# Scores of a head in six products, and half of an output projection side by side with two pairs of K tiles by seven products

## The chip, the cores and the metric

The kernel runs on one NeuronCore of a Trainium2 chip. Its engines run their own instruction streams and meet at semaphores: TensorE (PE in the profile, with PEld for its weight loads), VectorE (DVE), ScalarE (ACT), GpSimd (POOL) and SyncE (SP), which here does nothing but issue DMAs. The metric is the device time of one execution in microseconds (us); the times given are medians over runs. Single instructions, waits and transfers are read from the trace of one profiled execution, whose own time stands beside its span.

## What is computed

Two layers of a decoder over 256 tokens of width 2048, in float32:

```python
for l in range(DEPTH):                       # DEPTH = 2
    h = _rmsnorm(x, attn_norm_g[l])
    proj = h @ w_in[l]                       # q | k | v | gate_b | gate_c | conv_in, 1024 each
    q, k, v, gate_b, gate_c, conv_in = jnp.split(proj, splits, axis=-1)
    q = _rmsnorm(q.reshape(B, S, N_HEADS, 2, HEAD_DK), q_norm_g[l])      # 8 heads, 2 x 64
    k = _rmsnorm(k.reshape(B, S, N_HEADS, 2, HEAD_DK), k_norm_g[l])
    ...
    # per head two score matrices s_m = q_m k_m^T * scale + bias, causal softmax each,
    # p = p_0 - lam * p_1, then p @ v, norm, scale
    attn = _diff_attention(q, k, v, lam, rel_bias)
    ...
    conv = gate_b * _short_conv(gate_c * conv_in, conv_w[l])
    x = x + jnp.concatenate([attn, conv], axis=-1) @ w_out[l]            # 2048 x 2048
    hm = _rmsnorm(x, mlp_norm_g[l]) @ w_up[l]
    x = x + jnp.square(jax.nn.relu(hm)) @ w_down[l]
```

## The kernel before

**Products.** A float32 number is carried as two float32r tiles, a high part (a ScalarE copy that rounds) and a low part (a VectorE subtraction of the high part). A product of two such matrices is three matmuls, high x high, high x low and low x high (`TERMS`). In `linear` (L386, matmuls at L399) 128 rows of the contraction (a K tile) take 2 x 3 = 6 matmuls of 512 columns: two token blocks `t`, three terms. The chunk of 512 output columns accumulates in a pair of PSUM banks, a `mm2` tile; there are two such tiles (pool `mm`), taken in turn. Three more banks go by `bank(...)` and one by the tag `av`.

**Weights.** `Weights` (L300) holds a list of jobs, made by `plain` (L346). A job issues a load of 512 KB (two K tiles by 512 columns, tile `raw`, four buffers) on SP's queue and splits it: `whi` on ScalarE (L315), `wlo` on VectorE (L316), three buffers each. `take` (L370) makes jobs up to three ahead of the one in use. `work` (class `Background`) advances attention and norms by ticks between matmuls.

**Order of a layer's mixer** (L730). q, k, v of half the heads; the attention of those heads runs in ticks beside the next products; the same for the other half. Then gate C and the convolution input (`gc`, `ci`, `linear_t`, L405), then gate B (`gb`, four products of 256 columns of the model). After each gate B product, `joined` evicts it (a ScalarE copy `gb3l` at L435, a VectorE sum `gb3w` at L437), `gate` (L724) multiplies it with the convolution into `ys` (L726) and `in_parts` (L717) splits it into a part of `cat` (L720, L721). `cat` has four tiles of four K tiles each: two from attention, two from the gates. Then the output projection, chunk after chunk: `o` of chunk n is `linear` over all 16 K tiles, added into `xs[n]` at L800, and the norm of that chunk starts (`Norm.chunk`, transposes at L469).

**Scores** (`unit`, L609). For a head, q and k are held with both 64-wide halves m: `kT` has the high part of k in half m's rows and again in the other half's, `kL` has the low part and zeros, `qT[:, m]` has the high part in its own 64 rows and the low part in the other 64. So for each m and each token block t a product with `kT` and one with `kL` give the score: 8 matmuls, of 128 columns for t = 0 and 256 for t = 1.

**What sets the order.** TensorE's order is that of the program. VectorE, ScalarE, SP and GpSimd are put in order by the tile framework's scheduler when the program is built; each runs its list in order. SP's list holds the loads of the next stage too: two 1 MB loads of the MLP's weights (`uraw`, L830) stand in it after the eighth load of the projection; their memory is that of mixer tiles, and they wait for the last reader of `ys`, the `cat` split at L721 of the fourth gate B product.

**The MLP** (L838 on) already holds a scheme of seven products; it isn't touched.

Of the kernel before, what the change touches and what calls it, by code (L numbers as in the profile page):

```python
# [9 lines left out]
F32 = mybir.dt.float32  # L10
# [5 lines left out]
P = 128  # L16
# [19 lines left out]
NB2 = DFF // (KG * P)  # L36

# [81 lines left out]
def trunk(ctx: ExitStack, tc: tile.TileContext, x, w_in, w_out, conv_w, q_norm_g, k_norm_g,  # L119
# [19 lines left out]
    def bank(name):  # L139
        return ps.tile([P, CH], F32, tag="bank", name=name)  # L140
# [307 lines left out]
    class Norm:  # L448
# [59 lines left out]
        def factors(self):  # L508
# [7 lines left out]
            diag = small.tile([P, NT, P], F32, tag="diag", name="diag", bufs=1)  # L516
# [82 lines left out]
    def attention(l, qT, kT, kL, v, h0, dst, bias, tmp, pace):  # L599
# [9 lines left out]
        def unit(i):  # L609
            h = h0 + i  # L610
            s = tmp.tile([P, 2, 3 * P], F32, tag="s", name=f"s{h}", bufs=2)
            mx = small.tile([P, NT, 2], F32, tag="mx", name=f"mx{h}")
            su = small.tile([P, NT, 2], F32, tag="su", name=f"su{h}")
            sc = [bank(f"sc{h}_{m}") for m in range(2)]
            for flip in range(2):
                for k in (kT, kL):
                    for t in range(NT):
                        W, m = (t + 1) * P, t ^ flip
                        nc.tensor.matmul(
                            sc[m][:, OFF[t]:OFF[t] + W], qT[:, m, i, t * P:(t + 1) * P],  # L620
                            k[:, m, i, :W], start=(k is kT), stop=(k is kL))
            for t in range(NT):
                W = (t + 1) * P
                for m in range(2):
                    nc.vector.tensor_tensor_reduce(
                        out=s[:, m, OFF[t]:OFF[t] + W], in0=sc[m][:, OFF[t]:OFF[t] + W],
                        in1=bias[:, 2 * h + m, S - W:], op0=ALU.add, op1=ALU.max, scale=1.0,
                        scalar=-3.0e38, accum_out=mx[:, t, m:m + 1])
# [100 lines left out]

    def mixer(l, norm, loads):  # L730

        with ExitStack() as scope:
# [17 lines left out]
            for n in range(D // CH):  # L750
                weights.straight(w_out[l], 0, D // P, n * CH)
# [10 lines left out]
            for half in range(2):  # L762
# [10 lines left out]
                for t in range(NT):  # L773
# [5 lines left out]
                                     1 + half), 3 + 9 * half)  # L779
# [17 lines left out]
            for n in range(D // CH):  # L797
# [8 lines left out]
    A11, A21, A12, A22, S1, S2, S3, S4 = range(8)  # L806
# [480 lines left out]
```

## Time and profile before

| | |
|---|---|
| median of 3 runs | 2129.5 us (2128.94 to 2129.52) |
| profiled execution, own time | 2129.46 us |
| its span in the trace | 2127.7 us |
| instructions in the trace | 29217 |
| matmuls | 10919, TensorE busy 2122.8 us |
| VectorE, ScalarE busy | 1692.9 us (80%), 1355.9 us (64%) |
| output projection | from 299.4 to 389.4 us in layer 0, from 1357 us in layer 1 |

A row of groups reads: line of the kernel, engine, operation, tile written <- tiles read, shapes, count | busy us, mean ns of one | idle us of the engine just before them and who ended it. A row of a timeline reads: start us, length us, engine, line, operation, tiles, count, and in brackets the idle time before it and its releaser. A row of the chain reads: start, length, engine, tile, line, count. A row of DMA issues reads: tile, queue, count, KB each, us to landing. Matmuls overlap in their pipeline: the 389 ns of one are its latency, and the spacing of starts is what it costs.

### The profile page before, as it was taken

How to read it: one execution, taken by the hardware profiler on the slowest of the kernel's cores; microseconds unless marked ns; L12 is line 12 of the kernel's file. 1: busy time of each engine (PE TensorE's matmuls, PEld its weight loads, DVE VectorE, ACT ScalarE, POOL GpSimd, SP SyncE). 2: the span in 40 equal slices, each digit the busy share in tenths (PEclk: the TensorE clock that was granted, in tenths of full speed). 3: DMA queues.
4: the chain of work that ended last, by engine and by line, in shares of the span. 5: the costliest groups of instructions: out<-in, count | busy, mean ns of one | idle time of the engine just before them, and what ended most of it. 6: DMA issues, size and time to landing. Idle time of an engine off the chain costs nothing.

```text
span 2127.7 us, 29217 instructions
## 1 busy us (share of the span) xinstructions
PE 2122.8 (100%) x10919; PEld 1817.8 (85%) x10919; DVE 1692.9 (80%) x2328; ACT 1355.9 (64%) x1782; POOL 160.2 (8%) x226
## 2 busy tenths in 40 slices
PE   9999999999999999999999999999999999999999
PEld 8888888888888888888888888888888888888887
DVE  6777655798888888799766776557988888888997
ACT  6666545677777677666565765446777777675664
POOL 3110100000000000001101101000000000000110
PEclk9999999999999999999999999999999999999999
DMA  7555676687777777788656565756877777777993
GB/s 271 178 168 184 201 226 191 203 255 228 228 233 233 232 236 228 249 303 290 217 170 180 165 206 180 228 177 213 258 232 236 228 230 233 234 232 256 319 308 106
DMA packets 297742, 476.01 MB, mean 224 GB/s; under 512 B 12707, under 2 KB 193781, under 8 KB 297600
## 3 DMA queue, kind: packets, MB, share of 16 engines
q1 hardware_dynamic: 269120, 406.76, 61.0%
q0 software_dynamic: 28288, 67.24, 9.9%
q8 instruction: 85, 1.39, 0.3%
q14 instruction: 57, 0.47, 0.1%
q10 hardware_dynamic: 192, 0.15, 0.0%
HBM read 440.52 MB, written 33.58 MB: 223 GB/s over the span
## 4 chain that ended last, share of the span: by engine, by line
PE 100%; DVE 0%; DVEq 0%; issue 0%
PE upc L974 31%; PE pr L1017 14%; PE o L399 8%; PE dn L1098 8%; PE ci L423 4%; PE gc L423 4%; PE gb L423 4%; PE q L399 4%; PE k L399 4%; PE v L399 4%; PE dn L1180 2%; PE dn L1017 2%; PE pr1r L1017 2%; PE pr0r L1017 1%; PE up L974 1%; PE upw L974 1%
## 5 line engine op out<-in xcount | busy, mean ns | idle before, releaser
L316 DVE TENSOR_TENSOR wlo<-raw,whi 128x1024 fp32r<-128x1024 f32 x274 | 331.9, 1223 | 221.8 <-ACT whi L315 154.7
L315 ACT ACTIVATE whi<-raw 128x1024 fp32r<-128x1024 f32 x274 | 290.3, 1060 | 287.6 <-PE o L399 67.9
L974 PE MATMUL upc<-nT,uhi 128*128 128x512 f32 x1920 | 454.7, 389 | 0.0
L974 PEld LDWEIGHTS upc<-nT,uhi 128*128 128x128 f32 x1920 | 360.3, 188 | 74.7
L838 DVE TENSOR_TENSOR ulo<-uraw,uhi 128x1024 fp32r<-128x1024 f32 x256 | 311.8, 1221 | 119.6 <-ACT f L1006 89.4
L837 ACT ACTIVATE uhi<-uraw 128x1024 fp32r<-128x1024 f32 x256 | 270.5, 1057 | 159.8 <-PE upc L974 137.3
L974 PEld LDWEIGHTS upc<-nT,ulo 128*128 128x128 f32 x1920 | 246.2, 191 | 9.3
L974 PE MATMUL upc<-nT,ulo 128*128 128x256 f32 x1920 | 249.1, 283 | 0.0
L399 PE MATMUL o<-whi,cat 128*128 128x512 f32 x512 | 159.5, 390 | 0.0
L1098 PE MATMUL dn<-whi,fb 128*128 128x512 f32 x496 | 156.5, 389 | 0.0
L863 ACT ACTIVATE b2h<-draw 128x1024 fp32r<-128x1024 f32 x83 | 88.2, 1063 | 48.4 <-PE pr L1017 41.3
L315 ACT ACTIVATE whi<-uraw 128x1024 fp32r<-128x1024 f32 x62 | 65.9, 1062 | 81.8 <-PE dn L1098 62.7
L399 PEld LDWEIGHTS o<-whi,cat 128*128 128x128 f32 x512 | 96.2, 188 | 19.7
L1098 PEld LDWEIGHTS dn<-whi,fb 128*128 128x128 f32 x496 | 93.1, 188 | 19.4
L984 ACT ACTIVATE ev<-upc 128x512 f32<-128x512 f32 x120 | 72.0, 600 | 54.3 <-PE upc L974 54.3
L863 ACT ACTIVATE t24h<-t 128x1024 fp32r<-128x1024 f32 x83 | 88.2, 1063 | 22.8 <-PE pr L1017 15.9
L864 DVE TENSOR_TENSOR t24l<-t,t24h 128x1024 fp32r<-128x1024 f32 x83 | 101.1, 1218 | 1.7
L864 DVE TENSOR_TENSOR b2l<-draw,b2h 128x1024 fp32r<-128x1024 f32 x83 | 100.9, 1215 | 1.1 <-ACT b2h L863 1.1
L864 DVE TENSOR_TENSOR t13l<-t,t13h 128x1024 fp32r<-128x1024 f32 x83 | 101.0, 1217 | 0.7
L877 DVE TENSOR_TENSOR t<-draw 128x1024 f32<-128x1024 f32 x83 | 101.1, 1218 | 0.3
L399 PE MATMUL o<-wlo,cat 128*128 128x512 f32 x256 | 99.7, 389 | 0.0
L863 ACT ACTIVATE t13h<-t 128x1024 fp32r<-128x1024 f32 x83 | 88.4, 1065 | 13.3 <-DVE t L877 2.9
(408 smaller groups left out, 4146.4 us busy)
## 6 DMA issues: line engine op xcount, KB each, us to landing
uraw<-in_w_up_dram SPq DMA_DIRECT2D x128, 1024.0 KB, 6.2
raw<-in_w_in_dram SPq DMA_DIRECT2D x191, 512.0 KB, 3.9
draw<-in_w_down_dram SPq DMA_DIRECT2D x174, 512.0 KB, 5.4
raw<-in_w_out_dram SPq DMA_DIRECT2D x64, 512.0 KB, 4.1
uraw<-in_w_down_dram SPq DMA_DIRECT2D x62, 512.0 KB, 6.2
raw<-in_w_down_dram SPq DMA_DIRECT2D x10, 1024.0 KB, 5.5
hid0p<-f POOLq DMA_DIRECT2D x19, 512.0 KB, 3.6
fb<-hid0p POOLq DMA_DIRECT2D x19, 512.0 KB, 7.6
```

The costliest lines, as they stand in the source:

```text
L315: pair = (nc.scalar.activation(hi, raw, AF.Copy), nc.vector.tensor_sub(lo, raw, hi.bitcast(F32)))
L316: nc.vector.tensor_sub(lo, raw, hi.bitcast(F32)))
L399: nc.tensor.matmul(acc[:, t], a.ap[:, pa, k % KG, t * P:(t + 1) * P], (hi, lo)[pw][:, j], start=(k == 0 and n == 0), stop=(k == nk - 1 and ...
L423: nc.tensor.matmul(acc[:, f, 0] if part else acc[:, f], wt[:, k % 4, fs], a.ap[:, 0, k % KG] if part else a.ap[:, :, k % KG], start=(part ...
L837: pair = (nc.scalar.activation(hi, src, AF.Copy), nc.vector.tensor_sub(lo, src, hi.bitcast(F32)))
L838: nc.vector.tensor_sub(lo, src, hi.bitcast(F32)))
L863: keep(nc.scalar.activation(hi, src, AF.Copy))
L864: keep(nc.vector.tensor_sub(lo, src, hi.bitcast(F32)))
L877: keep(nc.vector.tensor_sub(t[:, 0:2], raw[:, :, 1], raw[:, 0]))
L974: nc.tensor.matmul(acc[:, 0] if part else acc, wt[part][:, k], a.ap[:, 0, k % KG] if part else a.ap[:, :, k % KG], start=(part == 0 and kh ...
L1017: nc.tensor.matmul(prods[n], f[:, pa, a], b[pw], start=(start and m == 0), stop=(stop and m == 2))
L1098: nc.tensor.matmul(prods[p], f[:, pa, 2 * k + t], b[pw][:, n], start=(p in starts and k == 0 and m == 0), stop=(stop and k == 1 and m == 2))
```

## The change

Three edits. First, the scores of a head. The high part of q (both halves, each in its own 64 rows) is copied into one tile `both` by two ScalarE copies, and for each token block one matmul of `both` with `kL` of both m at once (256 or 512 columns) and two matmuls of `qT` with `kT` (one for each m) accumulate in one bank per token block: six products. The attention of a half starts two ticks sooner and waits two ticks after the copies.

Second, the first 1024 columns of the output projection are computed side by side: both `mm2` tiles are open at once and each pair of K tiles is multiplied with 512 columns of chunk 0 and of chunk 1 before the next pair. At the end chunk 0 takes its last two pairs first, then chunk 1.

Third, two of the eight pairs of K tiles (4 and 5, the first two gate B products, `GATED`) are multiplied as 2 x 2 blocks by seven products instead of eight: sums of the gated rows are made after gate B (`sums_of`), sums of the weights beside the projection (`jobs`), and the seven results are joined at the end of the second seven. The seven take the three `bank` tiles and the `av` tile. In the norm's factors, the tile `diag` moves into the pool of `wide` tiles.

```diff
-            diag = small.tile([P, NT, P], F32, tag="diag", name="diag", bufs=1)
+            diag = wide("diag")[:, :NT * P].rearrange("p (t c) -> p t c", t=NT)
...
         def unit(i):
             h = h0 + i
+            both = tmp.tile([P, S], F32R, tag="both", name=f"both{h}", bufs=1)
+            for m, r in enumerate(HALF):
+                nc.scalar.activation(both[r], qT[r, m, i].bitcast(F32), AF.Copy)
+            yield 2
...
-            sc = [bank(f"sc{h}_{m}") for m in range(2)]
-            for flip in range(2):
-                for k in (kT, kL):
-                    for t in range(NT):
-                        W, m = (t + 1) * P, t ^ flip
-                        nc.tensor.matmul(
-                            sc[m][:, OFF[t]:OFF[t] + W], qT[:, m, i, t * P:(t + 1) * P],
-                            k[:, m, i, :W], start=(k is kT), stop=(k is kL))
+            sc = []
+            for t in range(NT):
+                W, mine = (t + 1) * P, slice(t * P, (t + 1) * P)
+                sc.append(bank(f"sc{h}_{t}")[:, :2 * W].rearrange("p (m c) -> p m c", m=2))
+                nc.tensor.matmul(sc[t], both[:, mine], kL[:, :, i, :W],
+                                 start=True, stop=False, skip_group_check=True)
+                for m in range(2):
+                    nc.tensor.matmul(sc[t][:, m], qT[:, m, i, mine], kT[:, m, i, :W],
+                                     start=False, stop=(m == 1), skip_group_check=True)
...
+    class BySeven:
+        def __init__(self, l, bpool, weights):
...
+            n = D // (4 * P)
+            seven = [n + q for q in GATED]
+            plain = [i for i in range(2 * n) if i not in seven]
+            self.order = [("pair", plain[0])]
+            for i, j in zip(plain[1:], seven):
+                self.order += [("pair", i), ("seven", j)]
+            self.order += [("pair", i) for i in plain[1 + len(seven):-2]]
+            self.order += [(n, i) for n in range(2) for i in plain[-2:]]
...
+        def sums_of(self, q, y):
...
+            nc.vector.tensor_add(v[:, 0], a21, a22)
+            nc.vector.tensor_sub(v[:, 1], v[:, 0], a11)
+            nc.vector.tensor_sub(v[:, 2], a11, a21)
+            nc.vector.tensor_sub(v[:, 3], a12, v[:, 1])
+            hi, lo = (self.sums[GATED.index(q)][:, part] for part in range(2))
+            nc.scalar.activation(hi, v, AF.Copy)
+            nc.vector.tensor_sub(lo, v, hi.bitcast(F32))
+
+        def jobs(self, w, i):
...
+            def plain():
+                raws = []
+                for n in range(2):
+                    raw = self.weights.pool.tile([P, 2, CH], F32, tag="raw", name="raw", bufs=RAW)
+                    nc.sync.dma_start(
+                        raw, w[2 * P * i:2 * P * (i + 1), n * CH:(n + 1) * CH].rearrange(
+                            "(k p) c -> p k c", p=P))
+                    raws.append(raw)
+                mine["raw"] = raws
+                b11, b21 = two(self.pool, "b", "w7b", raws[0])
...
+                return b11, b21, split(hi[:, 0], lo[:, 0], raws[1][:, 1])
+
+            def sums():
+                left, right = mine["raw"]
+                t = mine["t"] = self.pool.tile([P, 4, CH], F32, tag="b", name="w7t")
+                nc.vector.tensor_sub(t[:, 0], right[:, 0], left[:, 0])
+                nc.vector.tensor_sub(t[:, 1], right[:, 1], right[:, 0])
+                made = two(apool, "a", "w7x", t[:, 0:2])
+                nc.vector.tensor_add(t[:, 2], t[:, 1], left[:, 0])
+                nc.vector.tensor_sub(t[:, 3], left[:, 1], t[:, 2])
+                return made
+
+            def more():
+                return two(apool, "a", "w7y", mine["t"][:, 2:4])
...
+        def project(self, cat, norm):
+            both = [mm.tile([P, NT, CH], F32, tag="mm2", name=f"o{self.l}{n}") for n in range(2)]
...
+            def seven(i, start, end):
...
+                b11, b21, b22 = weights.take()
+                t1, t3 = weights.take()
+                t2, t4 = weights.take()
+                for n, a, b in ((1, A11, b11), (2, A12, b21), (3, S4, b22), (5, S1, t1),
+                                (7, S3, t3), (6, S2, t2), (4, A22, t4)):
...
+                    for m, (pa, pw) in enumerate(TERMS):
+                        nc.tensor.matmul(prods[n], form(i, pa, a), b[pw], ...)
...
+                    if i == steps[-1]:
+                        x11, x21, x12, x22 = (xs[n][:, t] for n in range(2) for t in range(NT))
+                        e1, e2, e3, e4 = wide("e1"), wide("e2"), wide("e3"), wide("e4")
+                        nc.scalar.activation(e1, prods[1], AF.Copy)
+                        nc.vector.tensor_add(e2, prods[6], e1)
+                        nc.vector.tensor_add(e4, prods[5], e2)
+                        nc.vector.tensor_add(x22, prods[5], x22)
+                        nc.vector.tensor_add(e3, prods[7], e2)
...
+                    if j == done:
+                        onto(0)
+                        for x_, e in ((x11, e1), (x12, e4), (x21, e3), (x22, e3)):
+                            nc.vector.tensor_add(x_, x_, e)
+            onto(1)
+            for n in range(2):
+                work.start(norm.chunk(n, 2), 2 * n + 2)
...
-                                     1 + half), 3 + 9 * half)
+                                     1 + half), 1 + 9 * half)
...
                 gate(q, acc, cv, cat[2 + q // 2], ys[:, q])
+                if q in GATED:
+                    by_seven.sums_of(q, ys[:, q])
...
-            for n in range(D // CH):
+            by_seven.project(cat, mnorm)
+            for n in range(2, D // CH):
                 acc = linear(f"o{l}{n}", cat, weights)
```

With the numbers of `order`, the first half of the projection runs: pair 0, pair 1, seven 4, pair 2, seven 5, pair 3, then pairs 6 and 7 for chunk 0 and pairs 6 and 7 for chunk 1.

More of the change, by code (lines that the diff above doesn't have):

```diff
@@ L36 @@
 NB2 = DFF // (KG * P)
+GATED = (0, 1)
 SEVEN_AT = ((2, 4, 6, 8, 11, 13, 15, 17, 20, 22, 24),
@@ L749, in mixer @@
                 weights.turned(w_in[l], 3 * AW + q * WC)
-            for n in range(D // CH):
+            by_seven = BySeven(l, bpool, weights)
+            for what, i in by_seven.order:
+                if what == "seven":
+                    weights.jobs += by_seven.jobs(w_out[l], i)
+                    continue
+                for n in ((0, 1) if what == "pair" else (what,)):
+                    weights.plain(w_out[l], 2 * P * i, n * CH, 2)
+            for n in range(2, D // CH):
                 weights.straight(w_out[l], 0, D // P, n * CH)
@@ L794, in mixer @@
                 gate(q, acc, cv, cat[2 + q // 2], ys[:, q])
+                if q in GATED:
+                    by_seven.sums_of(q, ys[:, q])
             mnorm = Norm(1, l)
-            for n in range(D // CH):
+            by_seven.project(cat, mnorm)
+            for n in range(2, D // CH):
                 acc = linear(f"o{l}{n}", cat, weights)
```

71 lines of the change are left out of this document (69 added, 2 removed).

## Prediction

> **What bounds the kernel now.** I read the page first: span, busy shares and the chain that ended last.
>
> ```profile
> span 2127.7 us, 29217 instructions
> PE 2122.8 (100%) x10919; PEld 1817.8 (85%) x10919; DVE 1692.9 (80%) x2328; ACT 1355.9 (64%) x1782; POOL 160.2 (8%) x226
> ...
> PE 100%; DVE 0%; DVEq 0%; issue 0%
> ```
>
> The chain is TensorE from end to end. So each matmul removed pays its full pitch, and each new wait of TensorE costs its full length: there is no slack to absorb one. VectorE at 80% has room on average, which says nothing yet of single moments. Next the chain in order of time, for pitches:
>
> ```profile
> 299.61 24.51 PE o L399 x108
> 324.12 0.87 PE tpn L469 x8
> 324.99 21.80 PE o L399 x96
> ...
> 421.07 5.54 PE upc L974 x32
> ```
>
> A 512-column matmul of the output projection takes 21.80/96 = 0.227 us. The 32 of the MLP are 16 of 512 columns and 16 of 256, so one of 256 takes (5.54 - 16 x 0.227)/16 = 0.119. Last the timeline of TensorE around one head's scores:
>
> ```profile
> 84.55 0.39 PE L399 MATMUL q<-whi,nT 128*128 128x512 f32 x1
> 84.78 0.39 PE L619 MATMUL sc<-kT,qT 128*128 128x128 f32 x2
> ...
> 85.47 0.39 PE L619 MATMUL sc<-kL,qT 128*128 128x128 f32 x2
> 85.70 0.39 PE L399 MATMUL q<-whi,nT 128*128 128x512 f32 x1
> ```
>
> Eight products fill 85.70 - 84.78 = 0.92 us, 0.115 each, though half have 128 columns and half 256: up to 256 columns the instruction is paid, not the column.
>
> **The change, part by part.**
>
> Scores. Six products a head: 256, 128, 128, 512, 256, 256 columns, so 0.227 + 5 x 0.117 = 0.81 us against 0.92: 0.11 saved, 1.8 us over 16 heads. Bounds: nothing (the columns are 1536 before and after) and 2 x 0.115 x 16 = 3.7; I keep 1.8, since both pitches are measured on neighbours. By the Trainium skill, TensorE: Matmul & The Clock Gate, section Back-to-back issue gap, a lone matmul costs its columns plus 2.5 ns; with equal columns the saving would be 0.1 us in all and the sum 1.7 us higher. The 0.115 us of the 128- and 256-column pairs above speaks against that.
>
> The two new copies of q halves per head stand on ScalarE. In the order of instructions of the changed program those of heads 1 to 7 are queued right behind the release by the head before, some 50 matmuls (11 us) or more ahead of their use, so I cost them at nothing; the weight copies on the same engine cover them. Without the cover a head would pay two copies, bounded by the 0.47 us of a 128x256 one (first fence below).
>
> Seven products. Two K pairs a layer take 21 instead of 24 matmuls: 2 x 2 x 3 x 0.227 = 2.7 us saved. The same bytes are loaded by the same number of loads. New on VectorE are the sums and splits, at these durations:
>
> ```profile
> L283 ACT ACTIVATE nT<-tpn,gains 128x256 fp32r<-128x256 f32 x32 | 13.6, 467 | 8.8 <-DVE nT L284 8.8
> L316 DVE TENSOR_TENSOR wlo<-raw,whi 128x1024 fp32r<-128x1024 f32 x274 | 331.9, 1223 | 221.8 <-ACT whi L315 154.7 <-issue 47.6 <-PE gc L423 8.4
> L880 DVE TENSOR_TENSOR t<-t,draw 128x512 f32<-128x512 f32 x83 | 56.7, 684 | 0.0
> L1001 DVE TENSOR_TENSOR h<-h 128x128 f32<-128x128 f32 x60 | 17.0, 283 | 0.0
> ```
>
> One seven takes 3 x 1.22 + 5 x 0.68 = 7.1 us of VectorE for 21 x 0.227 = 4.8 us of TensorE, where a plain pair takes 2.4 for 5.4. The sums of the gated rows (4 x 0.28 + 0.68 each) fall into the gate-B stage and its idle 3.26 us (next fence). The eight additions at the end (8 x 0.68 = 5.5) lie beside the 48 matmuls (10.9 us) after the second seven, with four splits: 10.4 of 10.9, nothing on the path; uncovered, the third chunk's start would wait. The four PSUM banks that the seven holds cost nothing: the last attention transposes stand before gate B.
>
> Now the order of work around the start of the projection, before:
>
> ```profile
> 298.74 2.36 DVE L316 TENSOR_TENSOR wlo<-raw,whi 128x1024 fp32r<-128x1024 f32 x2 [3.26 <-issue]
> 301.02 0.68 DVE L437 TENSOR_TENSOR gb3w<-gb,gb3l 128x512 f32<-128x512 f32 x1
> 301.81 0.69 DVE L726 TENSOR_TENSOR ys<-gb3w,cv 128x512 f32<-128x512 f32 x1
> 303.49 1.23 DVE L316 TENSOR_TENSOR wlo<-raw,whi 128x1024 fp32r<-128x1024 f32 x1 [0.99 <-ACT whi L315]
> 304.63 0.68 DVE L721 TENSOR_TENSOR cat<-ys,cat 128x512 fp32r<-128x512 f32 x1
> ```
>
> ```profile
> 297.78 1.06 ACT L315 ACTIVATE whi<-raw 128x1024 fp32r<-128x1024 f32 x1 [0.75 <-PE gb L423]
> 299.64 0.60 ACT L435 ACTIVATE gb3l<-gb 128x512 f32<-128x512 f32 x1 [0.81 <-PE gb L423]
> ...
> 317.36 1.06 ACT L315 ACTIVATE whi<-raw 128x1024 fp32r<-128x1024 f32 x1 [3.02 <-DMA raw<-in_w_out_dram]
> ```
>
> ```profile
> 295.51 0.37 SPq L356 DMA_DIRECT2D raw<-in_w_out_dram  x1
> 299.99 0.37 SPq L356 DMA_DIRECT2D raw<-in_w_out_dram  x1
> 305.39 0.99 SPq L830 DMA_DIRECT2D uraw<-in_w_up_dram  x2
> 307.51 1.58 SPq L356 DMA_DIRECT2D raw<-in_w_out_dram  x1
> ...
> SPq L830 <- DVE cat L721: 0.2, 1, 0.2
> ```
>
> And the DMA view of single issues (at 295.51, 305.39, 307.51), whose last column is the time to landing:
>
> ```profile
> raw<-in_w_out_dram SPq DMA_DIRECT2D x1, 512.0 KB, 4.8
> uraw<-in_w_up_dram SPq DMA_DIRECT2D x2, 1024.0 KB, 8.7
> raw<-in_w_out_dram SPq DMA_DIRECT2D x1, 512.0 KB, 9.7
> ```
>
> **First wait.** Side by side means that chunk 1 takes the accumulator which still holds gate B's last product, so the 13th matmul waits for its eviction gb3w. Before, chunk 1 came 22 us later. In the changed order the first seven's split w7b stands ahead of both halves of that eviction. Its rows are the load of 295.51: landed 300.3, copied 301.4, low part 302.6 (1.22), gb3w 303.3. The matmul is due at
>
> ```profile
> 299.44 0.40 PE L399 MATMUL o<-whi,cat 128*128 128x512 f32 x1
> ```
>
> plus 12 x 0.227 = 302.2. Wait: 1.1 us. Had the rows landed long before, 298.74 + 2.28 + 1.14 + 0.68 = 302.84 would still leave 0.7.
>
> **Second wait.** Two MLP loads of 1 MB each go out when VectorE has made the last cat part (the wait row above), and SP issues in order. In the changed program the second seven's two loads are behind them, and on VectorE the cat part is behind most of the first seven. Back to back an operation starts 0.08 us before the end of the one ahead, so 1.14 and 0.60 each. The right-hand rows of the first seven (load of 299.99) land at 304.8; then t1, t2-type sums (two of 0.60), the gate product, a split, a sum, a split, cat: 304.8 + 5 x 0.60 + 2 x 1.14 + 0.08 = 310.2. Before it ended at 305.3. So the 2 MB leave 4.9 us later, and what follows them lands at 307.51 + 9.7 + 4.9 = 322.1.
>
> TensorE reaches the second seven after 24 + 24 + 21 + 24 = 93 matmuls, at 299.44 + 21.1 + 1.1 = 321.65. From there: copy of b 322.1 to 323.2, low part 324.4; then, in VectorE's order, two sums, a split of 512, a sum (2.4), the split of pair 3's first tile (1.14), a sum (0.60), low part of x 329.8; pair 3's second tile, low part of y 332.1. Product 5's second matmul takes the low part of x, so TensorE stands until 329.8; six matmuls on it needs y's low part, 332.1; five more (1.1): 333.2. Undisturbed it would be 321.65 + 4.8 = 326.4. Wait: 6.8 us in pieces, the longest some 2.7. If the loads were as early as before (317.2), the same order of VectorE alone would leave 2.2; two us more of contention make 8.8. Afterwards pair 3 finds its tiles made.
>
> Layer 1 has the same order in the changed program and the same spacing before:
>
> ```profile
> 1358.47 0.68 DVE L437 TENSOR_TENSOR gb3w<-gb,gb3l 128x512 f32<-128x512 f32 x1
> ...
> 1362.08 0.68 DVE L721 TENSOR_TENSOR cat<-ys,cat 128x512 fp32r<-128x512 f32 x1
> ```
>
> 3.61 us apart as in layer 0. So both waits count twice. Sum, on the profiled execution's 2129.46 us (0.04 under the median 2129.5 of the runs): 2129.46 - 1.8 - 2.7 + 2 x (1.1 + 6.8) = 2140.8.
>
> **Rivals.** A measurement tells about 0.2% (4.3 us) from no change.
>
> *The clock falls in the broken stretch.* At its start the kernel's matmuls ran slower:
>
> ```profile
> 1.05 5.05 PE L173 MATMUL warm<-ones 128*128 128x128 f32 x22 [1.05 <-DVE mhalf L165]
> ```
>
> 0.23 us each, against 0.87/8 = 0.109 for the 128x128 transposes above. If the second wait brought this back for about as long (5 us of matmuls at twice the pitch, 2.5 lost, on both sides of the stretch), each layer pays 2.5 to 5: 2146 to 2151. For it: TensorE would be busy for under half of 11.6 us. Against: no piece is longer than some 2.7 us. By the Trainium skill, TensorE: Matmul & The Clock Gate, Part 1, an idle window of about 3.4 us halves the clock; by that rule it stays up, and no run here shows it.
>
> *The waits are hidden: faster.* In the trace of before the same 2 MB delay a load by 9.7 us, ScalarE waits 3.02 for it, and TensorE does not. If the second seven's rows land by 315 and the sums run ahead, only the first wait or none is left: 2129.46 - 4.5 = 2125.0, up to 2127.2. It decides at y's low part being made before 325.3, 16 matmuls into the seven. Against: cat cannot end before about 310, as its chain starts with a landing at 304.8.
>
> *The loads are in time, the order of VectorE is not.* 2129.46 - 4.5 + 2 x (1.1 + 2.2) = 2131.6: no change by measure.
>
> *The scores gain nothing, or 3.7.* 2142.6 or 2138.9, inside the forecast.
>
> **How the numbers follow.** Forecast 0.72, clock 0.10, VectorE's order alone 0.10, hidden 0.08. Bounds: all costs low 2129.46 - 2.7 - 3.7 + 2 x (0.7 + 2.2) = 2128.9; all high 2129.46 - 2.7 + 2 x (1.1 + 8.8) = 2146.6; the forecast's own range 2136 to 2146. The range 2130 to 2149 leaves out the hidden case and the worst of the clock. Faster is 0.08, same 0.10, slower 0.82.
>
> **What would show it.** Per head six products in 0.81 us. Waits of TensorE at the 13th o matmul for gb3w, about 1 us; then, after 93, on the w7b copy, w7x and w7y, 6 to 7 us, twice. SP's first uraw after the projection's start about 10.8 us after the first o matmul, not 6. Wrong would be: rows of the second seven landing early, a dearer score stage (copies late on ScalarE), or matmuls at twice their pitch after the stretch.

## The result, and the profile after

| | before | after |
|---|---|---|
| median | 2129.51 us (2128.94 to 2129.89) | 2141.9 us (2139.95 to 2144.1) |
| profiled execution, own time | 2129.46 us | 2141.39 us |
| matmuls | 10919 | 10875 |

The changed kernel is slower: the ratio is 1.006, with a 95% interval of 1.0049 to 1.007. It has 44 matmuls fewer, 32 of the scores and 12 of the sevens. These are the page of the kernel after (span, busy time of the engines, the shares of the chain that ended last):

```profile
span 2139.6 us, 29236 instructions
PE 2122.5 (99%) x10875; PEld 1812.2 (85%) x10875; DVE 1724.6 (81%) x2388; ACT 1377.3 (64%) x1828; POOL 159.2 (7%) x226
...
PE 96%; DMA 2%; DVE 1%; issue 1%; ACT 0%; SPq 0%; DVEq 0%; ACTq 0%
```

Before, the chain was TensorE to 100%. Now 4% of it are something else, a DMA above all. The view of TensorE's waits (line, tile, releaser: us in total, times, longest) names where:

```profile
PE po L861 <- DVE w7x L781: 4.0, 2, 2.5
PE po L861 <- ACT w7b L780: 3.0, 2, 2.8
PE o L836 <- DVE gb3w L440: 1.9, 2, 1.1
PE po L861 <- DVE w7b L781: 1.5, 2, 0.8
PE po L861 <- DVE w7y L781: 1.2, 2, 0.6
```

Each is there twice, once a layer. `gb3w` is the wait at the 13th matmul of the projection, the other four belong to the second seven. None of them was in the trace of before. The rows of layer 0's first wait are the 12th and the 13th matmul:

```profile
300.78 0.39 PE L836 MATMUL o<-whi,cat 128*128 128x512 f32 x1
302.25 0.50 PE L836 MATMUL o<-whi,cat 128*128 128x512 f32 x1 [1.08 <-DVE gb3w L440]
```

The timeline of TensorE shows the second seven of layer 0 (first five rows) and of layer 1:

```profile
320.56 0.39 PE L836 MATMUL o<-whi,cat 128*128 128x512 f32 x1
323.73 0.50 PE L861 MATMUL po<-w7b,cat 128*128 128x512 f32 x1 [2.78 <-ACT w7b L780]
324.99 0.77 PE L861 MATMUL po<-w7b,cat 128*128 128x512 f32 x2 [0.76 <-DVE w7b L781]
...
330.27 1.43 PE L861 MATMUL po<-w7x,sf 128*128 128x512 f32 x5 [1.53 <-DVE w7x L781]
...
332.54 0.73 PE L861 MATMUL po<-w7y,sf 128*128 128x512 f32 x2 [0.61 <-DVE w7y L781]
```

```profile
1385.81 0.50 PE L861 MATMUL po<-w7b,cat 128*128 128x512 f32 x1 [0.23 <-ACT w7b L780]
1387.07 0.74 PE L861 MATMUL po<-w7b,cat 128*128 128x512 f32 x2 [0.76 <-DVE w7b L781]
...
1392.35 1.41 PE L861 MATMUL po<-w7x,sf 128*128 128x512 f32 x5 [2.47 <-DVE w7x L781]
...
1394.62 0.73 PE L861 MATMUL po<-w7y,sf 128*128 128x512 f32 x2 [0.63 <-DVE w7y L781]
```

Cut at the starts of matmuls, the two traces differ like this. The first matmul of layer 0's projection starts at 298.26 instead of 299.44 (0.9 of it the scores of eight heads; the rest is within what other kernels with these scores differ by, 298.02 to 298.75). From there to the first matmul of the MLP it takes 98.18 us instead of 89.76 in layer 0 (+8.42), and 95.38 instead of 89.76 in layer 1 (+5.62). From the first MLP to the second projection it is 0.97 shorter, and the tail is the same. Sum: -1.18 + 8.42 - 0.97 + 5.62 = +11.89, of the 11.93 between the two executions. Each projection has six matmuls less (1.36 us), so it holds 9.8 us of waits and slowed matmuls in layer 0 and 7.0 in layer 1.

The loads behind it, from SP's timeline (start, length, what it issues) and the DMA view (queue, count, KB, us to landing; the issues at 308.39 and 309.47):

```profile
308.39 0.99 SPq L1007 DMA_DIRECT2D uraw<-in_w_up_dram  x2
309.47 3.77 SPq L794 DMA_DIRECT2D raw<-in_w_out_dram  x2
```

```profile
uraw<-in_w_up_dram SPq DMA_DIRECT2D x2, 1024.0 KB, 9.6
...
raw<-in_w_out_dram SPq DMA_DIRECT2D x1, 512.0 KB, 13.1
```

The MLP's 2 MB leave 10.1 us after the first o matmul (5.95 before), the second seven's rows leave right behind them and need 13.1 us. They are there at 322.5, while TensorE has come to them at 320.8. In layer 1 the same rows (issued at 1374.64) need 10.0 us:

```profile
raw<-in_w_out_dram SPq DMA_DIRECT2D x1, 512.0 KB, 10.0
```

There they are there at 1384.6, 0.8 us before TensorE comes to them, and it waits all the same. From the landing VectorE's order sets the pace (layer 0):

```profile
323.71 1.23 DVE L781 TENSOR_TENSOR w7b<-raw,w7b 128x1024 fp32r<-128x1024 f32 x1 [10.55 <-ACT w7b L780]
...
329.00 1.22 DVE L781 TENSOR_TENSOR w7x<-w7t,w7x 128x1024 fp32r<-128x1024 f32 x1
330.13 1.22 DVE L319 TENSOR_TENSOR wlo<-raw,whi 128x1024 fp32r<-128x1024 f32 x1
331.27 1.22 DVE L781 TENSOR_TENSOR w7y<-w7t,w7y 128x1024 fp32r<-128x1024 f32 x1
```

It idled 10.55 us for the copy of those rows, and then needed until 332.5 for what TensorE wanted at once.

### The profile page after: what moved, and what is told of

The parts are those of the page before. It is cut to its first block, busy times and chain, and to the rows that moved or that the text cites. A ratio compares the mean times of both kernels' runs of the same rounds, so it can differ in the third digit from the quotient of the medians.

```text
span 2139.6 us, 29236 instructions
## 1 busy us (share of the span) xinstructions
PE 2122.5 (99%) x10875; PEld 1812.2 (85%) x10875; DVE 1724.6 (81%) x2388; ACT 1377.3 (64%) x1828; POOL 159.2 (7%) x226
## 4 chain that ended last, share of the span: by engine, by line
PE 96%; DMA 2%; DVE 1%; issue 1%; ACT 0%; SPq 0%; DVEq 0%; ACTq 0%
PE upc L1151 31%; PE pr L1194 13%; PE dn L1275 8%; PE ci L426 4%; PE gc L426 4%; PE k L402 4%; PE v L402 4%; PE o L402 4%; PE gb L426 4%; PE q L402 4%; PE dn L1357 2%; PE dn L1194 2%; PE o L836 2%; PE pr1r L1194 2%; DMA raw<-in_w_out_dram 1%; PE pr0r L1194 1%
## 5 line engine op out<-in xcount | busy, mean ns | idle before, releaser
L319 DVE TENSOR_TENSOR wlo<-raw,whi 128x1024 fp32r<-128x1024 f32 x266 | 322.3, 1223 | 187.8 <-ACT whi L318 117.7
L318 ACT ACTIVATE whi<-raw 128x1024 fp32r<-128x1024 f32 x266 | 281.6, 1060 | 246.4 <-issue 33.7
L1275 PE MATMUL dn<-wlo,fb 128*128 128x512 f32 x248 | 96.5, 389 | 0.0
L1194 PE MATMUL pr<-t13h,f 128*128 128x512 f32 x240 | 93.8, 391 | 0.0
L319 DVE TENSOR_TENSOR wlo<-uraw,whi 128x1024 fp32r<-128x1024 f32 x62 | 75.9, 1223 | 17.9 <-ACT whi L318 17.6
```

The costliest lines, as they stand in the source:

```text
L318: pair = (nc.scalar.activation(hi, raw, AF.Copy), nc.vector.tensor_sub(lo, raw, hi.bitcast(F32)))
L319: nc.vector.tensor_sub(lo, raw, hi.bitcast(F32)))
L1194: nc.tensor.matmul(prods[n], f[:, pa, a], b[pw], start=(start and m == 0), stop=(stop and m == 2))
L1275: nc.tensor.matmul(prods[p], f[:, pa, 2 * k + t], b[pw][:, n], start=(p in starts and k == 0 and m == 0), stop=(stop and k == 1 and m == 2))
```

## The experiments

Theory: the whole loss is the two waits, and both come from where work stands in VectorE's list and SP's list. Rivals: the scores or the side-by-side order cost something themselves; the sevens are too much for VectorE in any order; the clock.

### The scores alone, and all but the sevens

The first kernel is the one before with the first edit only. The second is the changed one with no pair by seven:

```diff
-GATED = (0, 1)
+GATED = ()
...
-                        for x_, e in ((x11, e1), (x12, e4), (x21, e3), (x22, e3)):
+                        for x_, e in ((x11, e1), (x12, e4), (x21, e3), (x22, e3)) if steps else ():
```

> The kernel before with the first edit alone (scores of a head in six products; the projection as before). Theory: 32 matmuls fewer at 0.115 us, the two wider ones dearer, the copies hidden: 1.8 us less than before, 2127.7. Rival A: matmuls are priced by columns, nothing gained: 2129.5. Rival B: each removed matmul gives its full pitch: 2125.8. Rival C: the copies are late and a head waits for them: above 2129.5.

> The changed kernel with no pair by seven products: six-product scores and the first 1024 columns side by side, all eight pairs plain. Theory: the waits come with the sevens alone (their splits stand ahead of gate B's last eviction, their sums delay the last cat part), so without them no wait is left and only the scores' gain shows: 2127.7, equal to the scores alone; the first uraw load leaves about 6 us after the first o matmul as before. Rival: opening both accumulators at once is enough for the first wait, whatever stands ahead of the eviction: 1.1 us per layer more, 2129.9.

The scores alone: 2127.36 us (2127.06 to 2127.89), 1.9 below the 2129.25 of the kernel before beside it, ratio 0.9991 (0.9982 to 1.0). All but the sevens: 2127.64 (2127.33 to 2128.93), ratio 0.9993 (0.9984 to 1.0002). The scores' gain is the 1.8 us of the pitches. The two differ by less than their spread, and in neither trace does TensorE wait in the projection. So the side-by-side order is free to within these 0.3 us, opening both accumulators at once makes no wait by itself (the rival of the second run), and everything above 2127.6 hangs on the sevens.

### The order of the sevens pinned, and the MLP loads on another queue

The first marks the splits and the sums of the sevens so that they keep the order in which the program writes them. The second moves two loads to GpSimd's queue.

```diff
-                nc.scalar.activation(hi, src, AF.Copy)
-                nc.vector.tensor_sub(lo, src, hi.bitcast(F32))
+                late(nc.scalar.activation(hi, src, AF.Copy))
+                late(nc.vector.tensor_sub(lo, src, hi.bitcast(F32)))
...
-                nc.vector.tensor_sub(t[:, 0], right[:, 0], left[:, 0])
+                late(nc.vector.tensor_sub(t[:, 0], right[:, 0], left[:, 0]))
...
```

```diff
-                        nc.sync.dma_start(
+                        (nc.gpsimd if i == 1 else nc.sync).dma_start(
                             raws[kh], w_up[l][kh * 8 * P:(kh + 1) * 8 * P,
```

> The changed kernel with the sevens' splits and sums kept in the order in which the program writes them; the work is the same. On VectorE the eviction of gate B's last product then stands ahead of the first seven's low part, and the last cat part ahead of the first seven's sums; the order of SP's loads and the order inside the second seven stay. Theory: the first wait goes (1.0 to 1.2 us a layer), and cat ends about 3 us sooner, so the MLP loads leave, and the second seven's rows land, about 3 us sooner: 2141.9 - 2 x (1.1 + 3) = 2133.7, range 2132 to 2137. Rival: the time of the landing does not matter, VectorE's order inside the second seven sets its end: only the first wait goes, 2139.7.

> The changed kernel with the two 1 MB MLP loads of that place issued from GpSimd's queue instead of SP's, so the second seven's rows no longer stand behind them in a queue; VectorE's order is nearly the same. Theory: the rows land 4 to 6 us sooner (315 to 318 instead of 320 to 322.5), TensorE still waits 1.1 at the first wait and 2 to 3 for VectorE's order: 2125.0 + 2 x (1.1 + 2.5) = 2132.2, range 2130 to 2135. Rival A: both queues share the same engines, the 2 MB delay the rows all the same: 2140 to 2142. Rival B: the order of VectorE inside the second seven costs the whole wait: 2140.

The pinned order took 2143.74 us (2142.68 to 2147.14; ratio 1.0071, 1.0058 to 1.0083), 1.8 more than the changed kernel, where theory and rival both said less. What it was built for happened: no wait for `gb3w` is left, and cat ends at 305.2 instead of 308.3. But the first seven's sums now stand behind cat (the first at 305.8 instead of 302.9), and splits of the next plain pair, which were not pinned, stand between them as in the changed kernel; `w7y` is done at 314.8 instead of 311.9. So now the first seven waits as well, from TensorE's timeline and the windows view (window, length, busy time of PE, PEld, DVE, ACT, POOL, then the granted clock):

```profile
313.62 0.51 PE L861 MATMUL po<-w7y,sf 128*128 128x512 f32 x1 [0.90 <-ACT w7y L780]
314.87 0.73 PE L861 MATMUL po<-w7y,sf 128*128 128x512 f32 x2 [0.75 <-DVE w7y L781]
```

```profile
312.40:315.70 3.30, 1.65 (x7) 0.88 (x6) 1.30 (x2) 1.06 (x1) 0.00 (x0) 1.00 1.07 398
315.80:319.10 3.30, 3.30 (x10) 2.56 (x9) 0.00 (x0) 0.92 (x1) 0.00 (x0) 0.50 0.89 340
319.20:322.50 3.30, 3.30 (x16) 2.71 (x15) 3.03 (x4) 0.84 (x3) 0.00 (x0) 1.00 0.08 31
```

And behind two waits of under 1 us the clock was at 0.50 for 3.4 us: TensorE, busy all the time, has 10 matmuls in that window and 16 in the next. This execution holds four such steps. The run says that a better start of the loads is not enough; it can't be read as a price of the landing.

The other queue took 2131.88 us (2131.03 to 2134.87; ratio 1.0014, 1.0006 to 1.0023), where the theory had 2132.2. The DMA view at the issues of the second seven's left rows (309.59) and right rows (310.19), both beside one of the 1 MB loads:

```profile
raw<-in_w_out_dram SPq DMA_DIRECT2D x1, 512.0 KB, 4.0
...
raw<-in_w_out_dram SPq DMA_DIRECT2D x1, 512.0 KB, 9.8
```

The left rows, issued no earlier than in the changed kernel, need 4.0 us instead of 13.1. So 10 of the 12.4 us that the change lost go with this edit. Not all of it need be the place of 2 MB in a queue: in the second seven the scheduler also put `w7x` ahead of a plain pair's split, which stands before it in the changed kernel. What is left is the first wait (1.6 us in both layers together) and 3.3 us for `w7x` and `w7y`, whose sums need the right rows.

### The order written out, with either queue

Here gate B's last eviction, its product and its cat part, the splits of the plain pairs and all of the sevens' work are pinned in program order, and the four sums of a seven stand ahead of the splits of x and y:

```diff
-                made = two(apool, "a", "w7x", t[:, 0:2])
-                nc.vector.tensor_add(t[:, 2], t[:, 1], left[:, 0])
-                nc.vector.tensor_sub(t[:, 3], left[:, 1], t[:, 2])
-                return made
+                late(nc.vector.tensor_add(t[:, 2], t[:, 1], left[:, 0]))
+                late(nc.vector.tensor_sub(t[:, 3], left[:, 1], t[:, 2]))
+                return two(apool, "a", "w7x", t[:, 0:2])
...
+            weights.pinned = range(len(weights.jobs), len(weights.jobs) + 22)
```

> The changed kernel with the order of ScalarE and VectorE written out from gate B's last product to the end of the second seven: eviction, gate product and last cat part first; then each seven's splits and all four sums, x's split, y's split, and only then the next pair's tiles. The work and the queue (SP) are the same. Theory: both waits are matters of VectorE's order. Eviction at 300.4, cat at 302.5 (5 us sooner), first seven's sums done and its rows' buffers free at 308.2, so the second seven's rows are issued at 308.3 with the MLP loads 6 us ahead of them, and land at about 316; x's low part at 322.4, y's at 323.5, due at 322.3 and 323: no more than 0.5 us of wait a layer, clock 1.0: 2125.0 to 2126.5. Rival A: the 2 MB of MLP loads keep the rows from landing before 319 whatever the order: 2 x 3 us, 2131. Rival B: the sevens cost VectorE more than the stretch can hold in any order: 2130 or more.

> The ordered kernel just described, with the two MLP loads issued from GpSimd's queue as well. Theory: when the order is right the queue has little left to give: within 0.5 us of the ordered kernel, 2125 to 2126. Rival: the queue is the greater cause: 2 us or more below the ordered kernel.

The written order took 2127.59 us (2125.68 to 2131.49; ratio 0.9995, 0.9987 to 1.0004): 14 us below the changed kernel with the same work on the same queues. So VectorE can hold the sevens, and rival B is out. The median is 1 us above the expected range, and the executions lie 6 us apart. What is left in its trace (an execution of 2129.6 us) are waits of 0.8 us for the tiles of the next pair and of 0.6 for `w7x`, twice each.

With GpSimd's queue beside it: 2138.26 us (2136.2 to 2138.59), 11 more, where the theory said the same and the rival less. Both missed. The second seven's left rows, in the written order and then with the other queue (issues at 307.22 and 306.95):

```profile
raw<-in_w_out_dram SPq DMA_DIRECT2D x1, 512.0 KB, 9.8
```

```profile
uraw<-in_w_up_dram POOLq DMA_DIRECT2D x2, 1024.0 KB, 11.5
...
raw<-in_w_out_dram SPq DMA_DIRECT2D x1, 512.0 KB, 12.1
```

The 2 MB now start 3 to 4 us ahead of those rows instead of beside them. Their two halves land after 8.5 and 14.5 us (11.5 is the mean), where the run with the queue alone had 8.8 and 12.1, and the rows need 12.1. Two of the 16 pieces of these loads came some 3 us after the others in this execution. Over both layers TensorE waits 2.4 and 0.8 us for copies and 1.5 and 1.7 for low parts, and the clock is halved in three steps. So the second queue let the rows pass where both were issued together, and not where the loads had a start; these two runs show no more. By the Trainium skill, DMA: Bandwidth & Descriptors, section Issuing engines are not separate DMA queues, starting DMAs on several engines saves issue time only. This run, which gained nothing, agrees with that; the run with the queue alone, with 4.0 us instead of 13.1 for the rows, does not.

### The price of an idle time

Both are the kernel with the scores' edit alone, with an idle time of TensorE put in after the second chunk of the projection. Nothing of the computation is left out.

```diff
                 acc = linear(f"o{l}{n}", cat, weights)
+                if n == 1:
+                    st = nat.tile([P, CH], F32R, tag="wide", name="stall")
+                    late(nc.vector.tensor_copy(st, acc[:, 1]))
+                    late(nc.scalar.activation(st, st.bitcast(F32), AF.Copy))
+                    nc.tensor.matmul(bank("idle")[:, :P], st[:, :P], st[:, :P], start=True, stop=True)
```

> The kernel before with the scores in six products (2127.4 us), and one idle time of TensorE put in per layer, after the second chunk of the output projection: a VectorE copy of a finished sum and a ScalarE copy of that, and a small matmul that waits for them (its product is used by nothing). Idle about 1.7 us each. In the traces so far the granted clock was halved for 3.413 us steps after a step of the same grid with 2.03 us or more of idle TensorE, and stayed where there were 2.04 or less. Theory: 1.7 us never reaches that: clock 1.0, every run at 2127.4 + 2 x 1.7 = 2130.8, with as little spread as before. Rival: any idle of that order can lose the clock: runs 1.6 or 3.2 us longer among them.

> The same with two VectorE copies and two other sums between them: idle about 2.9 us each. Theory: where the step's bounds fall decides. A step holds 2.03 us or more of a 2.9 us idle in about 3 of 4 cases; then 3.413 us at half clock cost some 15 - 8 = 7 matmuls, 1.6 us. Without drops 2127.4 + 2 x 2.9 = 2133.2; runs spread from there to 2136.4, most at one or two drops. Rival (only a whole step without work halves the clock; the Trainium skill, TensorE: Matmul & The Clock Gate, Part 1, speaks of an idle window of about 3.4 us): no drop in any run, all at 2133.2 with clock 1.0.

They took 2139.58 us (2138.62 to 2139.94) and 2141.34 us (2140.94 to 2142.91). Both idle times came out longer than meant. In the first kernel a weight split stood ahead of the copy on VectorE (first fence); the waits of both follow:

```profile
343.99 1.22 DVE L316 TENSOR_TENSOR wlo<-raw,whi 128x1024 fp32r<-128x1024 f32 x1 [1.49 <-ACT whi L315]
345.13 0.68 DVE L808 CAST stall<-o 128x512 fp32r<-128x512 f32 x1
```

```profile
PE idle L810 <- ACT stall L809: 7.3, 2, 3.7
```

```profile
PE idle L810 <- DVE stall L809: 9.1, 2, 4.5
```

So neither could show how little is enough to lose the clock. They do show its price where nothing hides it: 2139.58 - 2127.36 = 12.2 us for 7.3 us of idle, 2141.34 - 2127.36 = 14.0 for 9.1. In both 4.9 us are left over, and in both traces the clock is halved in three steps: at most 1.6 us a step, since the small matmul and the restart behind it are in the 4.9 too. At half clock the matmuls of 512 columns start 0.427 us apart, so a whole step holds 8 of them instead of 15, which is 1.6 us again. From the windows view of the shorter one:

```profile
345.90:349.20 3.30, 2.67 (x7) 2.19 (x8) 1.11 (x2) 1.88 (x5) 0.00 (x0) 0.50 0.54 159
349.30:352.60 3.30, 3.30 (x10) 2.52 (x10) 0.00 (x0) 0.28 (x1) 0.00 (x0) 0.50 0.00 0
352.70:356.00 3.30, 3.30 (x19) 2.79 (x18) 2.44 (x5) 2.27 (x5) 0.00 (x0) 1.00 0.06 4
```

### The MLP loads held back

The two 1 MB loads wait for the last reader of `ys`. One more reader near the end of the second seven's work holds them until about 320.3. The first pair of kernels writes the element into a new tile. In the written order the reader is this copy behind the last split; with the scheduler's order it is an addition of the element and the last sum, which came to stand just ahead of the last split:

```diff
+                made = two(apool, "a", "w7y", mine["t"][:, 2:4])
+                if i == D // (4 * P) + GATED[-1]:
+                    held = small.tile([P, 1], F32, tag="held", name="held", bufs=1)
+                    late(nc.vector.tensor_copy(held, self.ys[:, 3, 1, S - 1:]))
+                return made
```

> The ordered kernel (e5) with the two MLP loads held back: a copy of one element per partition from ys, put behind the second seven's last split on VectorE, keeps their memory, so they leave after that (about 320 instead of 303), behind the projection's loads. Theory: what was left of the waits in the ordered kernel is the 2 MB moving ahead of the rows of the next pair and of the second seven; without it these land 4 to 6 us after their issue at 307 to 309, and nothing waits: 2125.0 (2129.5 less 1.8 and 2.7), with runs within 1 us of each other. Rival: the MLP loads, now later, hold up the loads behind them and TensorE waits there instead: 2127 or more.

> The changed kernel with that hold alone, VectorE's order otherwise as the scheduler chose it: the second seven's rows no longer move behind the 2 MB. Theory: they land at about 316 instead of 320 to 322.5, before TensorE comes at 320.6; what remains is the first wait, 1.1 a layer, and some 0.3 for VectorE's order: 2125.0 + 2 x 1.4 = 2127.8, range 2127 to 2130; so of the 12 us lost over the ideal, most is the 2 MB. Rival: VectorE's order keeps most of the second wait: 2134 or more.

2136.64 us (2136.4 to 2138.64) and 2138.79 us (2138.53 to 2139.07): both far off, though in the first trace TensorE waits nowhere in the projection and in the second only for `gb3w`. Each of the second pair differs from its partner in one line:

```diff
-                    held = small.tile([P, 1], F32, tag="held", name="held", bufs=1)
+                    held = mine["t"][:, 0, :1]
```

> The same hold on the ordered kernel, but the copied element goes into a sum tile that is there already (w7t), so that no new tile of 4 bytes per partition shifts the memory behind it. In the run with the new tile no wait of TensorE was left, and yet 2136.6 us: a 512-column matmul of the projection took 0.233 to 0.235 us instead of 0.227, and the MLP's were longer too. Theory: that was the shifted memory; with the layout of the ordered kernel the pitch is 0.227 again, no wait is left, and the time is the ideal 2125.0, range 2124.5 to 2126. Rival: the pitch comes from the MLP loads being later or from the pinned order; then 2136 again.

> The changed kernel with that hold alone, without a new tile; VectorE's order as the scheduler chose it. Theory: pitch 0.227; the second wait is gone, the first (0.9 to 1.1 a layer) is left: 2125.0 + 2 x 1.1 = 2127.2, range 2126.5 to 2128.5. So of the 17 us between the changed kernel and the ideal (2141.9 - 2125.0), some 15 hang on 2 MB of loads for the next stage. Rival: 2138.8 again, as with the new tile.

2126.93 us (2125.32 to 2129.06; ratio 0.9989, 0.998 to 0.9998) for the written order with the hold, and 2127.4 us (2126.95 to 2127.83; ratio 0.999, 0.9982 to 0.9999) for the changed kernel with the hold alone. The same 72 matmuls in the chain, with the new tile and without it:

```profile
325.12 16.80 PE o L847 x72
```

```profile
324.46 16.32 PE o L847 x72
```

0.233 us a matmul against 0.227. So a new tile of 4 bytes per partition cost 9.7 and 11.4 us over the kernel. That the tile does it is shown twice, since nothing else differs in either pair; that it does so by shifting the memory behind it is an inference, as no view shows addresses. Not all matmuls are longer: by the spacing of starts those of the projection and some of the MLP's are, and those of k and v are the same in both (0.232 and 0.231).

The last kernel is the test of the second wait: the changed kernel, VectorE's list left to the scheduler, and 2 MB of a later stage sent 12 us later. Its waits, the loads, and three rows of VectorE:

```profile
PE o L840 <- DVE gb3w L440: 1.7, 2, 1.1
PE warm L176 <- DVE mhalf L168: 1.1, 1, 1.1
PE q L402 <- DVE wlo L319: 0.3, 1, 0.3
```

```profile
308.65 0.97 SPq L794 DMA_DIRECT2D raw<-in_w_out_dram  x2
...
320.23 1.03 SPq L1012 DMA_DIRECT2D uraw<-in_w_up_dram  x2
```

```profile
317.92 1.22 DVE L781 TENSOR_TENSOR w7x<-w7t,w7x 128x1024 fp32r<-128x1024 f32 x1
...
319.85 1.23 DVE L319 TENSOR_TENSOR wlo<-raw,whi 128x1024 fp32r<-128x1024 f32 x1
320.99 1.22 DVE L781 TENSOR_TENSOR w7y<-w7t,w7y 128x1024 fp32r<-128x1024 f32 x1
```

The rows leave 0.8 us earlier than in the changed kernel and land at 313.0 and 314.2, not at 322.5; the waits of the second seven are gone, all of them, also those that end with VectorE. The first wait stays, 1.7 us in both layers. 2141.9 - 2127.4 = 14.5 us is what the hold is worth, and as much as the second waits of both layers took (8.5 and 6.0, below). But the scheduler did not choose the same list again: in the second seven the first two sums now stand ahead of `w7b`'s low part, and `w7x` ahead of the plain pair's split L319 that stands before it in the changed kernel. So the hold is not the only difference. By the rows it need not matter: `w7y` is done at 322.2 and TensorE takes its low part at 324.6, so one more split (1.14 us) ahead of it would still have been in time. That is an estimate; no run has the changed kernel's own list with early rows.

This kernel and the written order with the hold beat both kernels, by 2.0 and 2.4 us against the one before. Against the scores alone (2127.36) the first gains nothing and the second 0.4 us, less than its executions lie apart. In the first, 2.0 of the 2.7 us of the 12 matmuls saved go into the first wait (1.25 and 0.74 by the spacing of starts). In the second they come out only in the best executions (2125.32).

## Why the prediction was right

It said 2140.8 us, and 2141.9 were measured. Point by point:

| step | predicted | measured |
|---|---|---|
| scores | -1.8 | -1.9 (the scores alone) |
| 12 matmuls of the sevens | -2.7 | 12 fewer, pitch 0.227: -2.7 |
| first wait, a layer | 1.1 | 1.24 and 1.01 (spacing of starts less a pitch) |
| second wait, a layer | 6.8 | 8.5 and 6.0 (9.8 and 7.0 less the first wait) |

**Scores.** Six products cost their measured pitches, and the copies on ScalarE cost nothing. By the Trainium skill, TensorE: Matmul & The Clock Gate, section Back-to-back issue gap, equal columns would have left a gain of 0.1 us (an estimate by its formula); the measured 1.9 us speak against that. A head's six products take 0.806 us in the trace of the scores alone, where 0.81 was forecast. The even price of 0.115 us an instruction is right as a mean only: before, the next matmul starts 0.058 us after one of 128 columns and 0.17 after one of 256, and among the six the spacings go from 0.06 to 0.28.

**First wait.** Place, releaser and size are as predicted: the 13th matmul waits for `gb3w`, behind the first seven's low part on VectorE. Where the order was written out or pinned it was gone.

**Second wait.** Its three links held. The uraws left 10.1 us after the first o matmul (10.8 predicted, 5.95 before). The rows behind them landed 24.3 us after the first o matmul in layer 0 and 21.5 in layer 1 (22.7 predicted). From the landing to the end of y's low part it was 10.0 us (10.0 predicted). The 1.6 us too many and 1.2 too few at the landing account for the difference between the layers. That the two come out around the forecast is partly luck: in layer 0, 15 of the 16 pieces of that load were there at 318.6, and one came at 322.5, which the prediction did not foresee. Without it the wait of layer 0 would have been some 4.6 us instead of 8.5 (an estimate: 3.9 us off the landing) and this execution near 2137.5, still inside the forecast's range. Layer 1, with no such piece, is the cleaner test: 6.0 against 6.8.

**The term that was wrongly placed.** The prediction said that with the loads early VectorE's order alone would still leave 2.2 us a layer (its own steps give 328.3 - 326.4 = 1.9). That took the landing of before, 317.2, as the earliest. In the run with the hold alone the rows are there at 313.0 and 314.2, over 6 us ahead of TensorE's 320.8, and no such wait is left. Its list differs from the changed kernel's in the places of two sums and a split, so this shows that early rows and the scheduler's order go together without a wait, and for the forecast's exact list it is argued. The 2.2 was not part of the sum; it was the price of a rival and stood in the low bound.

**The rival of the clock** (0.10) has to be corrected. It did happen: at 325.55 in layer 0 the clock was halved for 3.4 us, as the windows view of the changed kernel shows.

```profile
322.10:325.50 3.40, 1.01 (x3) 0.66 (x4) 1.79 (x3) 1.93 (x3) 0.00 (x0) 1.00 0.07 25
325.60:328.90 3.30, 3.14 (x8) 1.96 (x6) 3.30 (x5) 3.09 (x4) 0.00 (x0) 0.50 0.23 54
329.00:332.40 3.40, 1.66 (x6) 1.05 (x6) 3.40 (x4) 2.12 (x2) 0.00 (x0) 1.00 0.83 261
```

It cost little there, because the matmuls that it slowed were followed by a wait for `w7x` until 330.2, which would have come anyway. The changed kernel's mean clock over an execution was 0.996 to 0.999, so all of the executions had such steps, more or fewer of them, and they lie 4 us apart (2139.95 to 2144.1) where those of before lie within 1. The prediction took the time of one drop, 2.5 us on both sides; a step costs 1.6 us, and only where no wait covers it. The Trainium skill's rule of an idle window of about 3.4 us (TensorE: Matmul & The Clock Gate, Part 1), by which the clock was to stay up, did not hold: the longest idle time was 2.78.

**The rival of no waits** had its price right: 2125.0 us, and the written order with the hold came to 2125.93 in its profiled execution with 0.5 us of wait left. Its condition, rows by 315, was met in both kernels with the hold that have no new tile. In layer 0 of the changed kernel they came 7 us later.

## What to carry to other kernels

Where TensorE is the whole chain, a saved matmul is worth its pitch, and an edit that adds work to VectorE is priced by what moves back in the lists of VectorE and of the DMA queue. Look for the last reader of memory that a later stage's big load waits for: when it moves, the load moves, and what stands behind that load in the queue may be needed sooner than the load is; holding 2 MB back by 12 us was worth 14.5 us here, with the list that the scheduler then chose. Compare that list too, row by row, before an edit is called the only difference. And compare the pitch of untouched matmuls of several stages in every run, before its time is read: a tile of 4 bytes more in a pool cost more than the edit saved.

## What was not expected of the hardware

**The clock goes by steps of 3.413 us on a grid that runs through the execution.** In all traces the granted clock changed, between the first and the last matmul, only at times that lie whole steps apart. A step ran at half clock after a step at full clock in which TensorE was busy for 1.05 us (changed kernel), 1.75, 1.27 and 1.86 (pinned), 1.61 (other queue), 1.63 and 1.47 (written order, other queue), 0.80 and less (put-in idle times). It stayed up after 1.57 and 1.66 (changed kernel), 1.93 (written order, other queue) and 2.23 and more, and in the last microseconds of kernels after 1.47 (written order with the hold and the new tile), 1.55 (written order) and 1.60 (before). So about half of a step idle, in pieces as well as in one, can be enough; between 1.47 and 1.86 us busy both happened, and the rows do not place the limit closer. To come back seems to take more: a step at half clock was followed by another one after 2.68 us busy (shorter idle time) and 2.73 (written order, other queue). Where the grid falls against a wait differs from execution to execution, which fits the spread of the kernels with waits. The Trainium skill, TensorE: Matmul & The Clock Gate, Part 1, gives the window as 3413 ns and free-running, and with that the traces agree.

**Some pieces of a load come late.** Of the 16 pieces of a load one or two landed 1.4 to 4 us behind the others, for several loads in a row around the second seven's rows: in layer 0 one in the changed kernel, in the pinned one and in the written order, and two with all but the sevens and in the written order with the other queue; in layer 1 one in the written order, two in the pinned one, with all but the sevens and in the written order with the other queue, and none in the changed kernel; none among the same loads of the kernel before. The Trainium skill, DMA: Bandwidth & Descriptors, section Latency and other measured facts, names two of the 16 DMA engines as usually slower; the trace does not say which engine a late piece belongs to, so this stays open.

**A new tile of 4 bytes per partition made the projection's matmuls 0.233 instead of 0.227 us**, without any wait in the views.
